# Feed-forward stream of a hybrid encoder layer: four inner tiles per PSUM sum, weights in 512-column units, a sixth of the low parts on GpSimd

## The chip, the cores and the metric

The kernel runs on one core of one Trainium2 chip. The metric is the device time of one execution in microseconds, and the time that is given is the median of several executions. The engines are TensorE (PE in the profile, with its weight loads as PEld), VectorE (DVE), ScalarE (ACT), GpSimd (POOL) and SyncE (SP), which issues the DMAs.

## What is computed

One layer: a feed-forward block, a mixing block with two kinds of attention side by side, a second feed-forward block, each between two RMS norms. All in float32.

```python
h = x + 0.5 * post1(SwiGLU_1(pre1(x)))
u = pre_mix(h)                      # multi-head latent attention and stick-breaking attention
h = h + post_mix(mix(u))            # 8 heads each, then one output projection
h = h + 0.5 * post2(SwiGLU_2(pre2(h)));  y = final(h)

def swiglu(x, w_gate, w_up, w_down):
    return (jax.nn.silu(x @ w_gate) * (x @ w_up)) @ w_down
```

D_MODEL is 1024, D_FF is 2816 (22 tiles of 128), and there are 1088 tokens: a prompt of 1024 and a sample of 64.

## The kernel before

The tokens are split into two groups: G1 with 576 tokens, moved through TensorE in two chunks of 288 columns, and G2 with 512 tokens in one chunk. Features lie on the partitions. Each float32 value is split into a high part that TensorE takes as it is (type float32r) and a low part, the rest; `mm3` (lines 159 to 162) computes one product as three matmuls, high by high, high by low and low by high. For weights the split is done on the chip: `weight` (lines 235 to 243) allocates a low and a high tile of 1024 columns, and for each half of 512 columns loads the raw values by DMA from SP's queue, casts them to the high part on ScalarE (line 121, `wh<-wr`) and subtracts on VectorE (line 122, `wl<-wr,wh`).

Two streams share TensorE. The feed-forward stream is `ffn` (lines 245 to 303), a generator that yields after each small step. The mixing stream is norms, projections, attention and the output projection. `weave` (lines 148 to 156) runs steps of the mixing stream and, in a ratio set stage by stage (`SHARE`, line 42), puts feed-forward steps between them. A planner then fixes the order of each engine's queue at build time by simulating the program with its own durations; each engine runs its queue in that order.

The order of work: the feed-forward block 1 of G1 alone; then mixing of G1 beside block 1 of G2; mixing of G2 beside block 2 of G1; then block 2 of G2 and the last norms. So `ffn` runs four times.

Inside `ffn` the 22 inner tiles are walked in parts of two. For an inner tile, the gate product (8 contraction tiles by 3 matmuls for each chunk) and the up product fill one PSUM bank each; ScalarE and VectorE form the silu (lines 289 to 293), and the result is split into `hh` and `hl`. The second product, `down`, runs one inner tile late, between the first and the second tile of the next part: it loads the two weight rows of the part, and for each of the 8 output tiles and each chunk sums the two inner tiles in a PSUM bank, six matmuls. The bank then goes into `y`: a copy on ScalarE in the first part (line 263), and an add on VectorE in the other ten parts (line 265, `y<-f,y`).

The feed-forward stream has four PSUM banks (`f`). Its SBUF ring is set in line 811: four raw tiles of 512 columns, four low and four high weight tiles of 1024 columns, three tiles each for `hh` and `hl`. The mixing stream has tiles of its own; its scores lie in one PSUM tile `s`, which is freed when the softmax or the scans of the stick-breaking weights (lines 520, 526 and 529, VectorE) have read it.

GpSimd does every second split of normalised inputs (line 122, `xl`, `ul`), some residual adds (line 234) and small memsets for the attention (lines 561, 562, 665, 711).

Of the kernel before, what the change touches and what calls it, by code (L numbers as in the profile page):

```python
# [7 lines left out]
F32 = mybir.dt.float32  # L8
# [7 lines left out]
P = 128  # L16
# [18 lines left out]
# token groups: (first token, tokens, chunk of the moving axis). The tokens lie as  # L35
# the first half of the prompt, the sample, the second half of the prompt.
# [4 lines left out]
# TensorE work of the feed-forward stream for one unit of the mixing stream's, part by part  # L41
# [8 lines left out]
class Layer:  # L50
    def __init__(self, tc, ctx, a):
# [33 lines left out]
        # keys and values: group 1 (prompt | new), group 2, cached  # L85
# [28 lines left out]
    # x = hi + lo exactly; without x, lo holds the value and is replaced in place  # L114
# [12 lines left out]
    # TensorE work is counted, for the interleaving of the two streams  # L127
# [15 lines left out]
    # a step without TensorE work in the first stream makes room for some of the second's  # L143
# [4 lines left out]
    # the steps of the first stream, with the second one's between them: self.share of its work each  # L148
# [15 lines left out]
    # a bank of the feed-forward stream  # L164
# [3 lines left out]
    # a bank of the mixing stream  # L168
# [10 lines left out]
    # sum of squares, tile by tile  # L179
# [9 lines left out]
    # 1 / sqrt(mean over all features + eps), on every partition, from the sums of squares  # L189
# [9 lines left out]
    # the same with the sums over the tiles left to TensorE (T at most 512)  # L199
# [10 lines left out]
    # tmp() gives [P, T] tiles  # L210
# [9 lines left out]
    # hi and lo of gain * src * r  # L220
# [7 lines left out]
    # y := res + gain * y * r, for one tile of features  # L228
# [15 lines left out]

    def ffn(self, pool, tmp, n, g, xhi, xlo, y, end=None, tail=None):
        nc, a = self.nc, self.a
        _, T, C = g
        wg, wu, wd = a[f"wg{n}"], a[f"wu{n}"], a[f"wd{n}"]
        pend = []
        order = [(dt, c0, C) for dt in range(KT) for c0 in range(0, T, C)]  # L250

        def down(part, first, order, beside=iter(())):
            ws = [self.weight(pool, wd[mi]) for mi, _, _ in part]
            for dt, c0, C in order:
                ps = self.bank_f()
                for i, ((wh, wl), (_, hh, hl)) in enumerate(zip(ws, part)):
                    self.mm3(ps[:, :C], wh[:, dt * P:dt * P + P], wl[:, dt * P:dt * P + P],
                             hh[:, c0:c0 + C], hl[:, c0:c0 + C], i == 0, i == len(part) - 1)
                yield True
                next(beside, None)  # L260
                yy = y[:, dt, c0:c0 + C]
                if first:
                    nc.scalar.copy(yy, ps[:, :C])
                else:
                    nc.vector.tensor_tensor(yy, ps[:, :C], yy, op=ALU.add)  # L265

        for m in range(0, FT, 2):
            part = []
            for mi in (m, m + 1):
                if mi > m and pend:  # L270
                    yield from down(pend.pop(0), m == 2, order)
                gh, gl = self.weight(pool, wg[mi])
                uh, ul = self.weight(pool, wu[mi])
                hh = pool.tile([P, T], F32R, name="hh")
                hl = pool.tile([P, T], F32R, name="hl")
                for c0 in range(0, T, C):
                    cs = slice(c0, c0 + C)
                    pg = self.bank_f()
                    for k in range(KT):
                        ks = slice(k * P, k * P + P)  # L280
                        self.mm3(pg[:, :C], gh[:, ks], gl[:, ks], xhi[:, k, cs], xlo[:, k, cs], k == 0, k == KT - 1)
                        yield True
                    pu = self.bank_f()
                    for k in range(KT):
                        ks = slice(k * P, k * P + P)
                        self.mm3(pu[:, :C], uh[:, ks], ul[:, ks], xhi[:, k, cs], xlo[:, k, cs], k == 0, k == KT - 1)
                        yield True
# [12 lines left out]
        if tail:  # L300
            order = [(dt, c0, tail) for c0 in range(0, T, tail) for dt in range(KT)]
        yield from down(pend.pop(0), False, order, end)
        self.run(end)

    # projections of the mixing block for the tokens of one group
    def project(self, gi, g, hi, lo, pool, ev, tmp):
# [14 lines left out]
        # query latent  # L321
# [13 lines left out]
        # rotary key: rows 64..95 the key, rows 96..127 its halves swapped  # L335
# [14 lines left out]
        # stick-breaking queries and keys, two heads per tile  # L350
# [16 lines left out]
        # latent attention: queries  # L367
        for m in range(2):
            # four heads: [query tile][head][128]
# [12 lines left out]
        # key/value latent  # L382
# [14 lines left out]
        # stick-breaking values, tokens on the partitions  # L397
# [17 lines left out]
        # latent attention: keys and values  # L415
# [3 lines left out]
    def cached(self, pool, ev, tmp):  # L419
        """keys and values of the cached latents"""  # L420
        nc, a = self.nc, self.a
        wh, wl = self.weight(pool, a["wukv"])
        cal = ev.tile([P, PAST], F32R, name="ll")
        cah = ev.tile([P, PAST], F32R, name="lh")
        ca = tmp()[:, :PAST]
        nc.sync.dma_start(ca, a["c_lat"])
        self.split(cah, cal, x=ca)
        yield from self.latent_kv(ev, tmp, wh, wl, cah, cal, PAST, PAST, 2)
# [25 lines left out]
    # ---- attention pieces  # L454
    def load_keys(self, pool, kind, h, parts):
        """hi and lo of the keys of one head on 128 rows."""
# [19 lines left out]
    def load_values(self, pool, pair, parts):  # L476
        """[128 keys, key tile, head, hi|lo, 64]"""
# [620 lines left out]
```

## Time and profile before

| what | value |
|---|---|
| median of three runs | 2368.2 us |
| the three runs | 2366.61, 2368.2 and 2371.72 us |
| span of the profiled execution | 2367.6 us |
| TensorE busy | 2283.5 us, 96% |
| VectorE busy | 1539.0 us, 65% |
| ScalarE busy | 1244.7 us, 53% |
| GpSimd busy | 93.6 us |
| mean granted TensorE clock | 0.993 of full speed |

The profiled execution has no time listed beside its span of 2367.6 us, from the first to the last instruction; the span lies inside the range of the three runs. The profile is one execution. Busy time of an engine is the union of its instructions; waits are idle time just before an instruction, put down to what released it last. A busy TensorE is not one at its peak, since matmuls overlap.

### The profile page before, as it was taken

To read this page: it belongs to the slowest core of one execution; us is meant where nothing else is said; L and a number is where in the kernel's file an instruction comes from. 1 tells how busy PE (TensorE), PEld (TensorE's weight loads), DVE (VectorE), ACT (ScalarE), POOL (GpSimd) and SP (SyncE) were. 2 spreads that over 40 slices of the span, in tenths; PEclk is the share of its full clock that TensorE was granted. 3 is DMA by queue.
4 is the path that set the end of the run, shared out by engine and by line. 5 is a ranking of instruction groups with operands and counts; after the bars stand their busy time and mean duration, and the time that the engine had idled before them with its cause. 6 is when DMAs were issued, how large, how long until landed. Compare 5 with 4: busy or idle time off the path is not lost.

```text
span 2367.6 us, 37687 instructions
## 1 busy us (share of the span) xinstructions
PE 2283.5 (96%) x13869; PEld 2033.4 (86%) x13869; DVE 1539.0 (65%) x2743; ACT 1244.7 (53%) x2459; POOL 93.6 (4%) x270
## 2 busy tenths in 40 slices
PE   8999999989999999999999999999999999999997
PEld 7999999879987777788778999998888888888885
DVE  5555555764277878855873488888878588555555
ACT  6543333453367777754542477777776455433333
POOL 1000000010000000000110000000000010000001
PEclk9999999999999999999999999999999999999998
DMA  6322222445453343343444632323221424333321
GB/s 210 97 95 90 81 80 90 148 144 168 161 150 113 110 129 100 95 151 111 151 142 160 188 96 79 99 72 99 72 86 62 144 81 139 128 98 98 98 90 36
DMA packets 186615, 268.81 MB, mean 114 GB/s; under 512 B 59216, under 2 KB 68048, under 8 KB 186400
## 3 DMA queue, kind: packets, MB, share of 16 engines
q1 hardware_dynamic: 186432, 266.41, 35.8%
q8 instruction: 110, 1.80, 0.3%
q14 instruction: 73, 0.60, 0.1%
HBM read 227.61 MB, written 40.88 MB: 113 GB/s over the span
## 4 chain that ended last, share of the span: by engine, by line
PE 69%; DVE 12%; ACT 9%; DMA 4%; issue 4%; SPq 1%; POOL 1%; DVEq 0%; ACTq 0%; POOLq 0%
PE f L133 46%; PE s L133 11%; PE v L133 6%; PE t L133 3%; PE t L137 2%; DVE a L526 2%; DVE a L529 1%; ACT wh L121 1%; DVE a L520 1%; ACT a L517 1%; DVE wl L122 1%; ACT a L518 1%; ACT a L519 1%; DVE y L265 1%; DVE e L224 1%
## 5 line engine op out<-in xcount | busy, mean ns | idle before, releaser
L133 PE MATMUL f<-xh,wh 128*128 128x288 f32 (+1 forms) x2112 | 695.3, 329 | 4.4 <-ACT xh L121 2.8
L133 PE MATMUL f<-xl,wh 128*128 128x288 f32 (+1 forms) x2112 | 694.3, 329 | 2.9 <-POOL xl L122 1.8
L133 PE MATMUL f<-xh,wl 128*128 128x288 f32 (+1 forms) x2112 | 692.8, 328 | 0.0
L121 ACT CAST wh<-wr 128x512 fp32r<-128x512 f32 x638 | 374.2, 617 | 524.9 <-PE f L133 376.5
L122 DVE TENSOR_TENSOR wl<-wr,wh 128x512 fp32r<-128x512 f32 x638 | 431.2, 698 | 233.0 <-ACT wh L121 208.7
L133 PEld LDWEIGHTS f<-xl,wh 128*128 128x128 f32 x2112 | 397.7, 188 | 33.7 <-POOL xl L122 3.4
L133 PEld LDWEIGHTS f<-xh,wh 128*128 128x128 f32 x2112 | 397.6, 188 | 33.3 <-ACT xh L121 3.3
L133 PEld LDWEIGHTS f<-xh,wl 128*128 128x128 f32 x2112 | 397.5, 188 | 28.1 <-issue 0.8
L133 PE MATMUL f<-hh,wh 128*128 128x288 f32 (+2 forms) x1072 | 350.7, 328 | 6.6 <-ACT hh L121 3.2
L133 PE MATMUL f<-hl,wh 128*128 128x288 f32 (+2 forms) x1072 | 350.7, 327 | 0.0
L133 PE MATMUL f<-hh,wl 128*128 128x288 f32 (+2 forms) x1072 | 349.9, 327 | 0.2 <-DVE wl L122 0.2
L265 DVE TENSOR_TENSOR y<-f,y 128x288 f32<-128x288 f32 (+2 forms) x488 | 247.9, 523 | 85.4 <-PE f L133 83.8
L133 PEld LDWEIGHTS f<-hh,wh 128*128 128x128 f32 x1072 | 201.7, 189 | 23.4 <-ACT hh L121 4.0
L133 PEld LDWEIGHTS f<-hh,wl 128*128 128x128 f32 x1072 | 202.1, 189 | 14.3 <-issue 1.0
L133 PEld LDWEIGHTS f<-hl,wh 128*128 128x128 f32 x1072 | 202.1, 189 | 13.8 <-issue 0.8
L293 DVE TENSOR_TENSOR act<-f,act 128x288 f32<-128x288 f32 (+1 forms) x132 | 70.0, 531 | 92.6 <-PE f L133 91.8
L564 DVE TENSOR_TENSOR pl<-t,ph 128x384 fp32r<-128x384 f32 (+1 forms) x160 | 101.2, 633 | 35.6 <-ACT ph L563 31.2
L563 ACT CAST ph<-t 128x384 fp32r<-128x384 f32 (+1 forms) x160 | 86.7, 542 | 57.2 <-PE t L137 54.7
L292 DVE TENSOR_TENSOR act<-f,act 128x288 f32<-128x288 f32 (+1 forms) x132 | 69.8, 529 | 66.5 <-ACT act L291 66.4
L137 PE MATMUL t<-c_ident,a 128*128 128x128 f32 x616 | 106.0, 277 | 2.7 <-ACT a L531 0.9
L133 PE MATMUL s<-kh,qh 128*128 128x256 f32 (+3 forms) x224 | 84.4, 378 | 24.0 <-DVE a L529 16.1
L121 ACT CAST hh<-act 128x288 fp32r<-128x288 f32 (+1 forms) x132 | 64.8, 491 | 66.0 <-DVE act L293 65.9
(312 smaller groups left out, 3464.7 us busy)
## 6 DMA issues: line engine op xcount, KB each, us to landing
wr<-in_wg SPq DMA_DIRECT2D x176, 256.0 KB, 2.9
wr<-in_wu SPq DMA_DIRECT2D x176, 256.0 KB, 3.0
wr<-in_wd SPq DMA_DIRECT2D x176, 256.0 KB, 3.2
wr<-in_win SPq DMA_DIRECT2D x44, 256.0 KB, 3.3
kl<-ks SPq DMA_DIRECT2D x64, 128.0 KB, 2.8
wr<-in_wout SPq DMA_DIRECT2D x32, 256.0 KB, 2.8
h<-y SPq DMA_DIRECT2D x16, 288.0 KB, 2.3
p<-in_xT SPq DMA_DIRECT2D x16, 256.0 KB, 3.4
```

Of the source, the lines that this page charges most:

```text
L121: nc.scalar.copy(hi, x)
L122: eng.tensor_tensor(lo, x, f(hi), op=ALU.subtract)
L133: self.nc.tensor.matmul(out, lhsT=lhsT, rhs=rhs, start=start, stop=stop)
L137: self.nc.tensor.transpose(out, x, ident)
L224: self.nc.vector.scalar_tensor_tensor(x, src(k), self.gain(name, k), r, op0=ALU.mult, op1=ALU.mult)
L265: nc.vector.tensor_tensor(yy, ps[:, :C], yy, op=ALU.add)
L292: nc.vector.tensor_tensor(s, pg[:, :C], s, op=ALU.mult)
L293: nc.vector.tensor_tensor(s, pu[:, :C], s, op=ALU.mult)
L517: nc.scalar.activation(av, z, AF.Abs)
L526: nc.vector.tensor_tensor_scan(a[:, j0:n - 1][:, ::-1], zz[:, ::-1], a[:, j0:n - 1][:, ::-1], BIG, op0=ALU.add, op1=ALU.subtract)
L563: nc.scalar.copy(ph[:, end:], tr[:, end:])
L564: nc.vector.tensor_tensor(pl[:, end:], tr[:, end:], f(ph[:, end:]), op=ALU.subtract)
```

## The change

`GROUP = 4`: the inner tiles are walked in parts of four (22 is five parts of four and one of two). A product of the second kind sums the four inner tiles of a part in one PSUM bank, with twelve matmuls, before the bank is added to `y`. It still runs between the first and the second tile of the next part, now half by half: four weight units of 512 columns for the output tiles 0 to 3, then four for 4 to 7. The last part has two inner tiles, as before, and is run by `down_last`.

Weights of the feed-forward stream are loaded by `unit`: one low tile, one high tile and one raw tile of 512 columns each. The ring has eight low and eight high tiles of 512 columns where it had four of 1024, and five tiles each for `hh` and `hl` where it had three.

The subtraction of a unit goes to GpSimd for the second half of the up weights of every odd inner tile (11 in a run of `ffn`) and for the fourth inner tile's unit in each half of `down` (10 in a run): 84 of 528 units over four runs. The mixing stream's weights keep `weight`.

`dynamic_dma_scratch_size=1024` is passed to the program's builder. Comments are taken out; line numbers below `GROUP` shift.

```diff
+GROUP = 4
+    def unit(self, pool, src, eng=None):
+        lo = pool.tile([P, 512], F32R, name="wl")
+        hi = pool.tile([P, 512], F32R, name="wh")
+        raw = pool.tile([P, 512], F32, name="wr")
+        self.nc.sync.dma_start(raw, src)
+        self.split(hi, lo, x=raw, eng=eng)
+        return hi, lo
...
-        def down(part, first, order, beside=iter(())):
-            ws = [self.weight(pool, wd[mi]) for mi, _, _ in part]
-            for dt, c0, C in order:
-                ps = self.bank_f()
-                for i, ((wh, wl), (_, hh, hl)) in enumerate(zip(ws, part)):
-                    self.mm3(ps[:, :C], wh[:, dt * P:dt * P + P], wl[:, dt * P:dt * P + P],
-                             hh[:, c0:c0 + C], hl[:, c0:c0 + C], i == 0, i == len(part) - 1)
-                yield True
-                next(beside, None)
-                yy = y[:, dt, c0:c0 + C]
-                if first:
-                    nc.scalar.copy(yy, ps[:, :C])
-                else:
-                    nc.vector.tensor_tensor(yy, ps[:, :C], yy, op=ALU.add)
+        def units(src, eng=None):
+            return [self.unit(pool, src[:, i:i + 512], e) for i, e in ((0, None), (512, eng))]
+
+        def product(part, ws, first, dt, c0, C):
+            ps = self.bank_f()
+            ks = slice(dt % H * P, dt % H * P + P)
+            for i, ((wh, wl), (_, hh, hl)) in enumerate(zip(ws, part)):
+                self.mm3(ps[:, :C], wh[:, ks], wl[:, ks], hh[:, c0:c0 + C], hl[:, c0:c0 + C],
+                         i == 0, i == len(part) - 1)
+            yield True
+            yy = y[:, dt, c0:c0 + C]
+            if first:
+                nc.scalar.copy(yy, ps[:, :C])
+            else:
+                nc.vector.tensor_tensor(yy, ps[:, :C], yy, op=ALU.add)
+
+        def down(part, first):
+            for half in range(2):
+                ws = [self.unit(pool, wd[mi][:, half * 512:half * 512 + 512], nc.gpsimd if i == 3 else None)
+                      for i, (mi, _, _) in enumerate(part)]
+                for dt in range(half * H, half * H + H):
+                    for c0 in range(0, T, C):
+                        yield from product(part, ws, first, dt, c0, C)
...
-        for m in range(0, FT, 2):
+        for m in range(0, FT, GROUP):
             part = []
-            for mi in (m, m + 1):
-                if mi > m and pend:
-                    yield from down(pend.pop(0), m == 2, order)
-                gh, gl = self.weight(pool, wg[mi])
-                uh, ul = self.weight(pool, wu[mi])
+            for mi in range(m, min(m + GROUP, FT)):
+                if mi == m + 1 and pend:
+                    yield from down(pend.pop(0), m == GROUP)
+                gw = units(wg[mi])
+                uw = units(wu[mi], nc.gpsimd if mi % 2 else None)
...
-    sizes = {"wr": 4, "wl": 4, "wh": 4, "hh": 3, "hl": 3}
+    sizes = {"wr": 4, "wl": 8, "wh": 8, "hh": GROUP + 1, "hl": GROUP + 1}
...
-    nc = bacc.Bacc("TRN2", target_bir_lowering=False, num_devices=1)
+    nc = bacc.Bacc("TRN2", target_bir_lowering=False, num_devices=1, dynamic_dma_scratch_size=1024)
```

## Rows read from the trace of the kernel before

**Rows 1.** The page's first part: busy time, share of the span, instructions.

```profile
PE 2283.5 (96%) x13869; PEld 2033.4 (86%) x13869; DVE 1539.0 (65%) x2743; ACT 1244.7 (53%) x2459; POOL 93.6 (4%) x270
```

**Rows 2.** Windows: from:to, length, busy us of each engine (instructions), PEclk, DMA, GB/s.

```profile
60.00:420.00 360.00, 360.00 (x2712) 359.46 (x2711) 191.60 (x378) 136.28 (x286) 5.28 (x4) 1.00 0.27 88
660.00:1020.00 360.00, 351.47 (x1807) 277.26 (x1805) 290.67 (x591) 262.09 (x597) 17.46 (x118) 1.00 0.39 115
1380.00:1860.00 480.00, 459.44 (x3261) 429.81 (x3260) 389.98 (x693) 340.53 (x607) 13.69 (x92) 1.00 0.28 87
2040.00:2280.00 240.00, 240.00 (x1061) 198.72 (x1060) 125.38 (x194) 81.12 (x144) 0.00 (x0) 1.00 0.30 96
```

**Rows 3.** Waits of TensorE in 660:1020 and 1380:1860: total us, times, longest.

```profile
PE s L133 <- DVE a L526: 6.5, 18, 0.6
...
PE s L133 <- DVE a L529: 15.8, 25, 2.0
PE f L133 <- DVE y L265: 0.4, 2, 0.3
```

**Rows 4.** Timeline of 1640:1655, VectorE and TensorE at one late scan: start, us, instruction.

```profile
1644.16 0.95 DVE L520 SCALAR_TENSOR_TENSOR a<-s,a 128x768 f32<-128x768 f32 x1
...
1645.37 0.75 DVE L606 SCALAR_TENSOR_TENSOR osq<-o,c_osg,osq 128x512 f32<-128x512 f32 x1
...
1647.22 1.01 DVE L529 TENSOR_TENSOR_SCAN a<-s,a 128x383 f32<-128x383 f32 x1
1648.14 1.16 DVE L265 TENSOR_TENSOR y<-f,y 128x288 f32<-128x288 f32 x3
...
1648.37 0.44 PE L133 MATMUL s<-kh,qh 128*128 128x448 f32 x1 [2.02 <-DVE a L529]
```

**Rows 5.** Groups by form: count, busy us, mean ns, idle before and its releaser.

```profile
L265 DVE TENSOR_TENSOR y<-f,y 128x288 f32<-128x288 f32 x320 | 139.1, 451 | 42.9 <-PE f L133 42.0
L265 DVE TENSOR_TENSOR y<-f,y 128x512 f32<-128x512 f32 x152 | 102.3, 684 | 38.6 <-PE f L133 38.0
L122 DVE TENSOR_TENSOR wl<-wr,wh 128x512 fp32r<-128x512 f32 x638 | 431.2, 698 | 233.0 <-ACT wh L121 208.7 <-DMA vs<-e 13.2 <-PE f L133 3.8
L133 PE MATMUL f<-hh,wh 128*128 128x288 f32 x704 | 209.4, 298 | 4.6 <-ACT hh L121 3.2 <-DVE y L265 0.9 <-DVE act L292 0.2
```

**Rows 6.** Windows of line 265 alone (VectorE busy us, instructions), the two attention stages.

```profile
660.00:1020.00 360.00, 37.72 (x56) 1.00 0.39 115
1380.00:1860.00 480.00, 51.62 (x122) 1.00 0.28 87
```

**Rows 7.** Windows of tile `wl` (PE, PEld, DVE busy us, instructions), the same stages.

```profile
660.00:1020.00 360.00, 129.21 (x326) 61.13 (x325) 54.41 (x81) 1.00 0.39 115
1380.00:1860.00 480.00, 210.56 (x710) 133.25 (x710) 61.29 (x92) 1.00 0.28 87
```

**Rows 8.** GpSimd's groups by form: two-input subtractions of 128x512.

```profile
L122 POOL TENSOR_TENSOR xl<-e,xh 128x512 fp32r<-128x512 f32 x4 | 6.2, 1554 | 17.1 <-ACT xh L121 17.1
L122 POOL TENSOR_TENSOR xl<-p,xh 128x512 fp32r<-128x512 f32 x4 | 5.3, 1320 | 88.0 <-ACT xh L121 88.0
```

**Rows 9.** Timeline of 1163:1168, GpSimd and VectorE.

```profile
1164.27 1.41 POOL L122 TENSOR_TENSOR xl<-tmp,xh 128x576 fp32r<-128x576 f32 x1 [3.01 <-ACT xh L121]
...
1163.79 0.68 DVE L265 TENSOR_TENSOR y<-f,y 128x512 f32<-128x512 f32 x1
1164.38 1.83 DVE L122 TENSOR_TENSOR wl<-wr,wh 128x512 fp32r<-128x512 f32 x1
...
1167.95 0.68 DVE L122 TENSOR_TENSOR wl<-wr,wh 128x512 fp32r<-128x512 f32 x1
```

**Rows 10.** Waits in GpSimd's queue in 660:1020, then the longest kind in 1380:1860.

```profile
POOL a L665 <- DVE a L520: 146.8, 28, 8.3
POOL ph L561 <- PE v L133: 37.5, 5, 14.4
...
POOL ph L561 <- PE v L133: 195.0, 24, 13.9
```

**Rows 11.** DMA issues: count, KB each, median us to landing.

```profile
wr<-in_wd SPq DMA_DIRECT2D x176, 256.0 KB, 3.2
```

More of the change, by code (lines that the diff above doesn't have):

```diff
@@ L248, in ffn @@
         wg, wu, wd = a[f"wg{n}"], a[f"wu{n}"], a[f"wd{n}"]
+        H = KT // 2
         pend = []
-        order = [(dt, c0, C) for dt in range(KT) for c0 in range(0, T, C)]
-        def down(part, first, order, beside=iter(())):
-            ws = [self.weight(pool, wd[mi]) for mi, _, _ in part]
-            for dt, c0, C in order:
-                ps = self.bank_f()
-                for i, ((wh, wl), (_, hh, hl)) in enumerate(zip(ws, part)):
-                    self.mm3(ps[:, :C], wh[:, dt * P:dt * P + P], wl[:, dt * P:dt * P + P],
-                             hh[:, c0:c0 + C], hl[:, c0:c0 + C], i == 0, i == len(part) - 1)
-                yield True
-                next(beside, None)
-                yy = y[:, dt, c0:c0 + C]
-                if first:
-                    nc.scalar.copy(yy, ps[:, :C])
-                else:
-                    nc.vector.tensor_tensor(yy, ps[:, :C], yy, op=ALU.add)
@@ new lines, in down, with down_last @@
+        def down(part, first):
[5 more added lines that the diff above has]
+                        yield from product(part, ws, first, dt, c0, C)
+        def down_last(part, step, beside):
+            ws = [[self.unit(pool, wd[mi][:, half * 512:half * 512 + 512]) for mi, _, _ in part] for half in range(2)]
+            if step:
+                order = [(dt, c0, step) for c0 in range(0, T, step) for dt in range(KT)]
+            else:
+                order = [(dt, c0, C) for dt in range(KT) for c0 in range(0, T, C)]
+            for dt, c0, n in order:
+                for _ in product(part, ws[dt // H], False, dt, c0, n):
+                    yield True
+                    next(beside, None)
@@ L278, in ffn @@
                     pg = self.bank_f()
[L279 to L282, printed above, removed]
                     pu = self.bank_f()
[L284 to L287, printed above, removed]
+                    for ps, ws in ((pg, gw), (pu, uw)):
+                        for k in range(KT):
+                            wh, wl = ws[k // H]
+                            ks = slice(k % H * P, k % H * P + P)
+                            self.mm3(ps[:, :C], wh[:, ks], wl[:, ks], xhi[:, k, cs], xlo[:, k, cs],
+                                     k == 0, k == KT - 1)
+                            yield True
                     s = tmp()[:, :C]
@@ L299, in ffn @@
         end = end() if end else iter(())
-        if tail:
-            order = [(dt, c0, tail) for c0 in range(0, T, tail) for dt in range(KT)]
-        yield from down(pend.pop(0), False, order, end)
+        yield from down_last(pend.pop(0), tail, end)
         self.run(end)
```

## The prediction

> **What bounds the kernel now.** I read the page's first part, then the windows by stage, then TensorE's waits in the stages where it is not full. The first says that TensorE is busy 96% of the span, 2283.5 of 2367.6 us, with VectorE at 65% [rows 1]. So all that any edit beside TensorE can give back is 84 us, unless the matmuls themselves become fewer, and they don't. The windows say where these 84 us lie: in the two stretches in which the feed-forward stream runs alone (60 to 420 and 2040 to 2280) TensorE is busy for every one of the 600 us [rows 2]. There nothing is to be had. In the attention stages it is busy 351.5 of 360 and 459.4 of 480 us, so 8.5 and 20.6 us are idle, 29.1 together [rows 2]; the remaining 55 us lie at the start, at the end and in the norms and projections between the stages.
>
> In the attention stages VectorE is the fullest engine after TensorE: 290.7 of 360 and 390.0 of 480 us, 81% in both [rows 2]. The waits name it: TensorE stood before the scores matmul, which needs the one tile `s`, until a scan of the stick-breaking weights had ended, for 6.5 and 15.8 us, 22.3 together [rows 3]. The timeline of one such wait shows how it arises. The scan of line 529 follows line 520, but VectorE does a headnorm multiplication of 0.75 us and other small work between them; the scan ends near 1648.2, three adds into `y` that had piled up follow at once, and TensorE has been standing for 2.02 us [rows 4]. VectorE's queue is late there, and TensorE pays, because its own order is fixed.
>
> **Part 1: half of the adds into y go.** Ten of eleven parts end in adds before, five of six after; the last part keeps its own. In two runs over G1, adds of 288 columns fall from 320 to 160; of G2's 152 adds of 512 columns, 80 go (block 1 has 80 and keeps 40, block 2 has 72 and keeps 32). That is 160 by 0.451 and 80 by 0.684 us, 72 and 55, together 127 us of VectorE's 1539 [rows 5]. The matmuls stay as many; only the place of start and stop moves. In the stretches without mixing this is hidden already: TensorE is full there, and the adds wait for TensorE, not it for them [rows 2, 5]. In the attention stages line 265 takes 37.7 and 51.6 us [rows 6], so 18.9 and 25.8 us go. A bank now lasts twelve matmuls instead of six before VectorE must empty it; TensorE's waits for that are only 0.4 us there [rows 3], so this is worth nothing by itself.
>
> **Part 2: 84 of 528 subtractions go to GpSimd.** VectorE loses 84 by 0.698, 59 us [rows 5]. GpSimd takes 1.32 to 1.55 us for the same shape [rows 8], so it gains 111 to 130 us on top of 93.6, which is little over a span of 2367. In the attention stages there are 81 and 92 such subtractions on VectorE [rows 7]; a sixth are 13 and 15, worth 9 and 10 us.
>
> Against this stands what the trace shows where both engines subtract at once. At 1164.27 GpSimd begins a subtraction of 1.41 us; the `wl` that VectorE begins at 1164.38 takes 1.83 us, where the same form alone takes 0.68 [rows 9]. The add into `y` just before it kept its 0.68 us. So a blocked piece costs VectorE up to 1.15 us more, against 0.7 saved. The bounds of a moved piece for VectorE are a gain of 0.70 (no meeting) and a loss of 0.45 (each one meets a `wl`). Units come in groups of four and are cast one behind the other, so meetings will be common; I take half, a gain of about 0.1 us a piece, and so nothing, and keep both ends for the range. The Trainium skill, in "SBUF — State Buffer", section "Who interferes with whom", gives this as a rule: a VectorE instruction with two SBUF inputs and a GpSimd instruction that reads SBUF exclude each other for the whole instruction. By that rule every such meeting would block, and those rows agree.
>
> GpSimd's queue is in order too, and behind its waits the moved piece would be late. It waits for the attention there, 5.2 us at a time on the commonest line (146.8 in 28), 14.4 at the longest [rows 10]. A group of four units of G2 lasts 48 matmuls at about 0.23 us, 11 us of TensorE's feed-forward work, and as that has some 70% of TensorE in this stage, an estimate from the timeline's pitch and the share of `f`, 16 us; a load (3.2 us [rows 11]), cast and subtraction take 5 of it. So 11 us are left, the usual wait fits, the longest misses by some 4 us. Cost 0 to 11 us (three misses); I take 0, since the usual wait is the nearest row. Queued behind a moved piece on GpSimd are the memsets for the attention; each may come up to 1.55 us later, and they run well before their readers.
>
> **Part 3: the rest.** Weights in units are the same bytes, loads, casts and subtractions; a unit's slots come free half a tile earlier, and nothing waits for it, so 0. SP's queue issues the same loads in the same number. Casts on ScalarE stay as many; copies of line 263 too. The first second product comes two inner tiles later: 0. A feed-forward step of twelve matmuls between mixing steps is coarser; its cost lies between a gain and a loss of about one step, 1.6 us, at each of the few stage changes, and I take 0. All instructions are planned anew, which shifts each queue a little: I give that 4 us either way, from the spread of 5.1 us that the three runs of one kernel have.
>
> **The sum.** In the attention stages VectorE's load falls by 18.9 + 9 and 25.8 + 10, less some 10 and 12 us for meetings (13 and 15 by about 0.8): to 273 of 360 and 366 of 480 us, 76% in both, from 81%. How waits shrink with that no row shows; between nothing (the waits come from chains that one engine runs in series) and all 22.3 us [rows 3]. As an estimate I take waits to go as load over idle share: 0.81/0.19 is 4.3, 0.76/0.24 is 3.2, a quarter less; without meetings (73%) a third. Of the 29.1 us idle [rows 2] this is 7 to 10, and I take 7. Start, end and stage changes: 0. The profiled span of 2367.6 lies 0.6 us under the median, so the forecast is 2368.2 - 7, 2361 us.
>
> What is late next is again the chain in VectorE's and ScalarE's queues behind one `s` tile: 520, 526 and 529 take some 3 us in series whatever else is queued [rows 4].
>
> **The rivals.**
>
> Nothing changes. TensorE is full where it was full, and the waits for the scans stay, since they come from scans that take longer than the planner believed, not from adds. For: in [rows 4] the adds stand behind the scan, not before it. Against: other pieces do stand between. Time 2368, give or take 4.
>
> A larger gain: the waits for the scans go altogether and the stage changes, which have VectorE chains too, shrink by some. 22.3 us less, 2346 us. For: both stages name VectorE almost alone [rows 3]. Against: the serial part of the chain stays.
>
> Slower: the meetings on the shared SBUF input. Place: the attention stages, 28 moved pieces, and the stage changes, where GpSimd has its large work. Price: if each blocked `wl` holds up the scan behind it for 1.15 us and TensorE waits for all of it, 32 us; less the 7 of the forecast, 25 us, 2393 us at the most; half of that is the likelier form, 2380. It decides when more than six of the 28 (7/1.15) hold up a scan on which TensorE waits. For: the stretch from 0.68 to 1.83 us is plain [rows 9]. Against: scans and adds read PSUM for one input, and the add beside GpSimd's work was not longer [rows 9], so only what stands directly behind a blocked piece suffers. It is the page's rule at its full price; by that rule alone, without the halved adds, the kernel would be slower.
>
> That the change does not do what it says: were the planner to bring GpSimd's pieces too late, TensorE would show waits for `wl` from GpSimd, up to 11 us; it is counted in the range.
>
> **How the numbers follow.** Forecast of a gain of 5 to 16 us: 0.42. Larger gain: 0.10. Nothing (within 0.2%, 4.7 us, which is about what a measurement can tell from no change here): 0.28. Slower: 0.20. So faster 0.52, same 0.28, slower 0.20. The likeliest case alone spans 2352 to 2363. The range for 8 in 10 leaves out most of the larger gain and the dear half of the slower case: 2349 to 2376.
>
> **What would show each step.** The group of line 265 with 248 instructions in all, and VectorE under 1400 us busy. GpSimd with 84 `wl` subtractions of 1.3 to 1.8 us, and single `wl` on VectorE of 1.2 to 1.9 us beside them. TensorE still full from 60 to 420. Its waits for lines 526 and 529 near 17 us instead of 22.3. I am wrong if VectorE's load in the attention stages falls as worked out and TensorE's idle time there does not; or if a wait of `f` for `wl` from GpSimd appears; or if the time moves in the stretches without mixing.

## The result, and the profile after

The changed kernel takes 2383.76 us (median of four runs, 2379.76 to 2386.27) where the kernel before takes 2368.24 (2366.61 to 2371.72): 15.5 us more, a ratio of 1.0058 with a 95% interval of 1.0044 to 1.0073. The profiled execution took 2381.92 us, with a span of 2380.1.

The first line of the page after, as in [rows 1]:

```profile
PE 2289.1 (96%) x13869; PEld 2036.3 (86%) x13869; DVE 1419.4 (60%) x2416; ACT 1267.6 (53%) x2462; POOL 206.7 (9%) x354
```

VectorE lost 119.6 us, and TensorE did not gain. For the same 13869 matmuls it is busy 5.6 us longer, and its idle time went from 84.1 to 91.0 us (span less busy time): 6.9 and 5.6 are the 12.5 us by which the two spans differ. What the 5.6 us are worth is taken up in the last section.

The windows after, columns as in [rows 2]:

```profile
60.00:420.00 360.00, 360.00 (x2714) 359.52 (x2713) 162.93 (x283) 143.12 (x291) 31.77 (x23) 1.00 0.28 88
660.00:1020.00 360.00, 349.98 (x1792) 273.81 (x1792) 267.03 (x541) 262.81 (x599) 34.57 (x131) 1.00 0.39 113
1380.00:1860.00 480.00, 458.76 (x3236) 427.14 (x3236) 361.83 (x611) 348.03 (x619) 30.24 (x105) 1.00 0.29 88
1860.00:2040.00 180.00, 168.06 (x910) 147.73 (x909) 119.78 (x187) 81.63 (x144) 23.23 (x15) 0.96 0.36 113
```

Where the feed-forward stream is alone, TensorE is still full. In the attention stages VectorE fell to 74 and 75%, and TensorE's idle time there rose, from 29.1 to 31.3 us. In the second stage change, from 1860 to 2040, TensorE is idle for 11.9 of 180 us, where the same window of before has 7.8; its granted clock there is 0.96 against 0.99, so more of that stretch stands at 1.2 GHz, the lower of its two levels. That window of before:

```profile
1860.00:2040.00 180.00, 172.18 (x919) 150.02 (x918) 126.30 (x203) 87.88 (x160) 12.65 (x8) 0.99 0.37 119
```

TensorE's longest waits after, over the whole span (total us, times, longest), then four of before:

```profile
PE s L136 <- DVE a L560: 15.4, 30, 1.1
...
PE s L136 <- DVE a L557: 6.3, 16, 0.7
PE f L136 <- DVE y L278: 6.2, 2, 5.9
PE s L136 <- DVE rx L190: 5.7, 1, 5.7
PE v L136 <- DVE tmp L190: 4.4, 2, 3.6
```

```profile
PE s L133 <- DVE a L529: 16.1, 26, 2.0
...
PE s L133 <- DVE a L526: 6.5, 18, 0.6
...
PE s L133 <- DVE rx L187: 2.2, 1, 2.2
PE v L133 <- DVE tmp L187: 2.2, 1, 2.2
```

The waits for the scans (lines 557 and 560 after, 526 and 529 before) are 21.7 us, and were 22.6; the 22.3 of [rows 3] leave out one wait of 0.3 us. What grew is single stalls at the stage changes: before a second-product matmul for an add into `y` (5.9 us), before the norm statistics `rx` (5.7) and `tmp` (3.6). The stall of 5.9 us in the timeline, VectorE first, then TensorE (start, us, instruction):

```profile
1933.55 0.46 DVE L278 TENSOR_TENSOR y<-f,y 128x288 f32<-128x288 f32 x1 [1.77 <-PE f L136]
1934.07 2.08 DVE L227 SCALAR_TENSOR_TENSOR e<-h,c_gains,rx 128x512 f32<-128x512 f32 x3
...
1939.19 3.08 DVE L227 SCALAR_TENSOR_TENSOR e<-h,c_gains,rx 128x512 f32<-128x512 f32 x3
...
1944.69 0.68 DVE L125 TENSOR_TENSOR xl<-e,xh 128x512 fp32r<-128x512 f32 x1
1945.30 1.54 DVE L278 TENSOR_TENSOR y<-f,y 128x288 f32<-128x288 f32 x4
...
1945.80 0.61 PE L136 MATMUL f<-hh,wh 128*128 128x288 f32 x1 [5.93 <-DVE y L278]
```

For eleven microseconds VectorE works through the scaling of the next norm (line 227 and its splits), which waits for GpSimd's splits in between. Four adds into `y` stand behind it in VectorE's queue, all four PSUM banks of the feed-forward stream are full, and TensorE stands.

### The profile page after: what moved, and what is told of

It reads as the page before. It is cut to its first block, busy times and chain, and to the rows that moved or that the text cites. A ratio compares the mean times of both kernels' runs of the same rounds, so it can differ in the third digit from the quotient of the medians.

```text
span 2380.1 us, 37747 instructions
## 1 busy us (share of the span) xinstructions
PE 2289.1 (96%) x13869; PEld 2036.3 (86%) x13869; DVE 1419.4 (60%) x2416; ACT 1267.6 (53%) x2462; POOL 206.7 (9%) x354
## 5 line engine op out<-in xcount | busy, mean ns | idle before, releaser
L124 ACT CAST wh<-wr 128x512 fp32r<-128x512 f32 x638 | 383.5, 618 | 507.1 <-PE f L136 343.3
L125 DVE TENSOR_TENSOR wl<-wr,wh 128x512 fp32r<-128x512 f32 x554 | 385.6, 709 | 242.9 <-ACT wh L124 206.2
L125 POOL TENSOR_TENSOR wl<-wr,wh 128x512 fp32r<-128x512 f32 x84 | 115.2, 1372 | 1136.0 <-ACT wh L124 1127.7
L136 PEld LDWEIGHTS f<-hl,wh 128*128 128x128 f32 x1072 | 202.4, 189 | 13.4 <-issue 0.5
L278 DVE TENSOR_TENSOR y<-f,y 128x288 f32<-128x288 f32 (+2 forms) x248 | 126.8, 519 | 109.1 <-PE f L136 108.5
L125 DVE TENSOR_TENSOR hl<-act,hh 128x288 fp32r<-128x288 f32 (+1 forms) x132 | 87.5, 663 | 43.0 <-ACT hh L124 42.5
```

What stands on the lines that cost most here:

```text
L124: nc.scalar.copy(hi, x)
L125: eng.tensor_tensor(lo, x, f(hi), op=ALU.subtract)
L136: self.nc.tensor.matmul(out, lhsT=lhsT, rhs=rhs, start=start, stop=stop)
```

## The experiments

Each run is beside runs of the kernel before on the same chip; "over before" is the difference of the two medians that were taken together. The kernel before had medians from 2367.3 to 2369.7 us on these occasions, so a difference between two runs of different occasions can shift by up to 2.4 us with the base that is used. e1 to e4 share one base, and so do e5 to e8, e9 and e10, e11 and e12, and e13 to e15.

| run | what it has | median, us | over before |
|---|---|---|---|
| the change | units, parts of four, GpSimd | 2383.8 | +15.5 |
| e2 | units, parts of two | 2379.0 | +11.6 |
| e1 | units, parts of four | 2370.0 | +2.7 |
| e3 | units, parts of two, GpSimd | 2392.0 | +24.6 |
| e4 | the change, other shares | 2384.9 | +17.6 |
| e5 | e1 and dummy subtractions on GpSimd | 2389.8 | +21.5 |
| e6 | e1 and memsets on GpSimd | 2377.0 | +8.7 |
| e7 | e1, GpSimd in the blocks alone | 2373.1 | +4.8 |
| e12 | e1, GpSimd beside mixing | 2383.4 | +13.7 |
| e8 | e2, adds first | 2371.8 | +3.5 |
| e9 | e1, adds first | 2371.1 | +3.8 |
| e10 | the change, adds first | 2376.3 | +9.0 |
| e11 | before, adds of 32 columns | 2378.2 | +8.5 |
| e13 | before, adds first | 2367.7 | -0.7 |
| e14 | e11, adds first | 2367.6 | -0.7 |
| e15 | e9, adds first at the residuals too | 2367.4 | -1.0 |

**The parts of the change.** Three runs take it apart: without GpSimd, with units alone, and with units and GpSimd but parts of two.

```diff
e1
-nc.gpsimd if i == 3 else None
-uw = units(wu[mi], nc.gpsimd if mi % 2 else None)
+None
+uw = units(wu[mi])
e2: e1 and
-GROUP = 4
+GROUP = 2
e3: the change and
-GROUP = 4
+GROUP = 2
-nc.gpsimd if i == 3 else None
+nc.gpsimd if i == 1 and half else None
```

> The changed kernel with its 84 subtractions back on VectorE; parts of four and units stay. Theory A (GpSimd's pieces hold up VectorE's two-input work in the serial chains at the stage changes; TensorE stands longer there and its clock falls to the lower level for some microseconds): 2366 to 2373 us, TensorE's stalls before rx and tmp at the stage changes (5.7 and 3.6 us in the changed kernel) back to about 2.3, granted clock at the lower level outside start and end for about 20 us instead of 24. Theory B (parts of four fall differently over the stage changes, so that adds into y queue behind the scaled chain and all four banks are full): still 2378 to 2386 us, with the 6 us stall before a second-product matmul near 1940 in place.

> Weights in units of 512 columns, but parts of two and nothing new on GpSimd. Theory A and B alike: within 0.2% of the kernel before, 2364 to 2373 us. If units themselves shift the plan so far that stalls move at the stage changes, it is off by more than 5 us, and neither theory is enough.

> Units, parts of two, and 84 subtractions on GpSimd (the up weights' second half of every odd inner tile, and the second inner tile's second half in the second product). Theory A: 2378 to 2386 us, as slow as the changed kernel. Theory B: 2364 to 2373 us, as the kernel before.

Without GpSimd: 2370.0 us, ratio 1.0011 (1.0001 to 1.0021). Units alone: 2379.0, ratio 1.0046 (1.0029 to 1.0063). Units and GpSimd with parts of two: 2392.0, ratio 1.0102 (1.0087 to 1.0117). So neither theory is enough. Units cost 11.6 us, parts of four on top of them give 8.9 back, and GpSimd costs 13.7 with parts of four (2383.8 against 2370.0) and 13.0 with parts of two. That these steps add up to about the 15.5 measured is no test, since each starts where the one before it ends; that GpSimd costs about as much with parts of two is one. Of Theory A's signs in e1, TensorE's wait before `tmp` is back at 2.1 us, but that before `rx` stays at 4.7 (2.2 before), and the granted clock from 1860 to 2040 at 0.96; so these two came in the main from something else than GpSimd's pieces.

Units alone were to change nothing. TensorE's wait in that run, and VectorE's queue ahead of it:

```profile
1929.94 0.46 DVE L278 TENSOR_TENSOR y<-f,y 128x288 f32<-128x288 f32 x1 [0.34 <-PE f L136]
...
1942.11 1.54 DVE L278 TENSOR_TENSOR y<-f,y 128x288 f32<-128x288 f32 x4
...
1942.62 0.61 PE L136 MATMUL f<-hh,wh 128*128 128x288 f32 x1 [9.53 <-DVE y L278]
```

It is the stall of the changed kernel, 9.5 us long. Eight adds stand behind the scaling here; in the kernel before, all but two of the sixteen are done when it begins. In the kernel before the same scaling meets another part of the feed-forward stream. The windows of the tiles `xh` (gate and up) and, of e2, `hh` (second product), from 1936 to 1942, columns as in [rows 2]; first before, then e2:

```profile
1936.00:1942.00 6.00, 6.00 (x32) 4.86 (x31) 2.99 (x3) 3.17 (x6) 3.15 (x3) 1.00 0.00 1
```

```profile
1936.00:1942.00 6.00, 0.00 (x0) 0.00 (x0) 0.00 (x0) 0.00 (x0) 0.53 0.00 0
```

Before, TensorE is full with gate and up products, whose banks last 24 matmuls each and need no add into `y`. In e2 it does nothing in these 6 us, and its granted clock is 0.53.

**Other shares.** The two shares of the attention stages were raised, to move the parts.

```diff
-SHARE = (0.1, 1.5, 0.1, 0.1, 1.2, 0.1)
+SHARE = (0.1, 1.6, 0.1, 0.1, 1.3, 0.1)
```

> The changed kernel with the shares of the feed-forward stream in the two attention stages at 1.6 and 1.3 instead of 1.5 and 1.2, so that parts of the feed-forward stream fall elsewhere over the stage changes. Theory A: 2378 to 2388 us, since the chains at the stage changes meet GpSimd's pieces anyway. Theory B: it moves by more than 5 us, to either side; the 6 us stall near 1940 is gone or is at another place.

2384.9 us, ratio 1.007 (1.0055 to 1.0085): the time did not move, and a stall of 5.2 us is there as before. TensorE's order did change, but only in the middle of the program; the part over the scaling stayed where it was. So the run speaks neither way.

**The adds first.** So the priority was changed instead: the feed-forward steps that are left are issued ahead of the scaling.

```diff
     def start2():
...
+        L.debt, L.pace = 96.0, 3.0
         yield from L.scaled(tmp, lambda k: h2[1][:, k], "pre2", rz[0], *x3)
+        L.pace = PACE
```

With units and parts of two (e8) TensorE's order stays as it is; VectorE takes eight adds into the scaled chain instead of behind it.

> Units with parts of two, and the feed-forward stream's remaining steps put ahead of the second norm's scaling (start2) in priority: on VectorE eight adds into y move from behind the scaled chain into it; TensorE's order stays. Theory B (units cost because a second product now lies over this chain and its four banks wait for the adds): the stall of 9.7 us is gone, and the time falls from 2379.0 to 2366 to 2371 us. Otherwise it stays at 2379.

2371.8 us, ratio 1.0012 (1.0002 to 1.0022): 7.2 us come back. VectorE in that run:

```profile
1937.62 0.69 DVE L125 TENSOR_TENSOR xl<-e,xh 128x512 fp32r<-128x512 f32 x1
1938.23 0.45 DVE L278 TENSOR_TENSOR y<-f,y 128x288 f32<-128x288 f32 x1
...
1939.92 1.17 DVE L278 TENSOR_TENSOR y<-f,y 128x288 f32<-128x288 f32 x3
...
1941.67 1.17 DVE L278 TENSOR_TENSOR y<-f,y 128x288 f32<-128x288 f32 x3
```

The adds are served in time, and no wait of `f` for `y` over 0.9 us is left in this stage change. 3.5 us of the units' cost stay unexplained.

The same line in three other kernels: parts of four without GpSimd (e9), the change (e10), and the kernel before as control (e13).

> Parts of four, units, nothing of the weights on GpSimd, and the feed-forward stream's remaining steps ahead of the second norm's scaling. If halving the adds is worth what the forecast said (7 us) once neither GpSimd nor the place of the second product costs anything: 2361 to 2365 us, faster than the kernel before by 0.1 to 0.3%, and 7 us under the units with parts of two in the same order (2371.8). If parts of four helped only because their banks fill more slowly under the scaled chain (9 us between 2379.0 and 2370.0), nothing is left of it: 2368 to 2372 us.

> The changed kernel with the feed-forward stream's remaining steps ahead of the second norm's scaling. The 6 us stall near 1940 goes: 2376 to 2380 us, and the distance to the same kernel without GpSimd's pieces stays 12 to 15 us if GpSimd's cost is spread over the other chains; if it sat in this one chain, both come out alike.

> The kernel before with the same priority for the remaining feed-forward steps ahead of the second norm's scaling. In it TensorE does gate and up products under that chain, so there is no stall of adds to take away. If the line helps only by that stall: 2364 to 2371 us, no change. If the line is a gain by itself: under 2362 us.

The control does not move: 2367.7, ratio 0.9998 (0.9989 to 1.0007). Parts of four come to 2371.1, ratio 1.0015 (1.0006 to 1.0024): no faster than e1, and where parts of two are with the same line. So the gain of 7 us does not come out. The time of e9 fits the second expectation, but not for the reason given there. TensorE's longest waits in this stage change of e1 show why:

```profile
1911.11 0.61 PE L136 MATMUL f<-hh,wh 128*128 128x288 f32 x1 [4.72 <-DVE y L278]
...
1939.96 0.58 PE L136 MATMUL f<-xh,wh 128*128 128x288 f32 x1 [2.90 <-DVE y L278]
```

In e1 the second product lies earlier than in e2 and in the change: most of it over the residual steps ahead of the norm, where TensorE waits for 4.7 us, and it ends 3 us after the scaling has begun. e9 has the same order of matmuls as e1. The new line takes its wait of 2.9 us away; the wait of 4.7 stays, and one of 4.2 for `hh` comes. So much of the 8.9 us that parts of four gave back is another place of the second product. A bank that lasts twice as long was compared only where that product lies over the scaling in both, with GpSimd's pieces: the stall is 9.5 us with parts of two (e3) and 5.9 with parts of four (the change). What halving the adds alone is worth in time stays open.

The change comes to 2376.3, ratio 1.0039 (1.0026 to 1.0053): 7.4 us less, and 5.2 over e9, not the 12 to 15 expected. From 1860 to 2040 TensorE is idle for 12.1 us in e9 and for 5.5 in e10, which keeps the change's order of matmuls and has none of e9's two long waits. So the 5.2 us understate GpSimd's pieces.

**GpSimd's share.** Dummy work on GpSimd, with all weights from VectorE: subtractions of the same operands that nobody reads (e5), or two memsets (e6).

```diff
-        self.split(hi, lo, x=raw, eng=eng)
+        self.split(hi, lo, x=raw)
+        if eng:
+            junk = pool.tile([P, 512], F32, name="junk")
+            eng.tensor_tensor(junk, raw, f(hi), op=ALU.subtract)
e6
+            eng.memset(junk, 0.0)
+            eng.memset(junk, 0.0)
```

> Parts of four, units, all subtractions back on VectorE, and GpSimd does 84 subtractions of the same operands into a spare tile that nobody reads. So GpSimd takes as long and reads as much as in the changed kernel, but no weight comes from it. Theory A (what costs is that VectorE's two-input instructions wait while GpSimd reads): 2380 to 2390 us, at least as slow as the changed kernel, since VectorE keeps its own 84 pieces too. Theory C (what costs is weights that come late from GpSimd's queue): 2367 to 2373 us, as the kernel with nothing on GpSimd (2370).

> As the dummy subtractions, but GpSimd writes two memsets of 512 columns each in their place and reads nothing. Theory A: 2367 to 2373 us, since nothing is read beside VectorE. If any work in GpSimd's queue costs (its own memsets for the attention come later, or the plan moves): 2376 us or more.

The dummy subtractions cost 19.8 us over e1 (2389.8, ratio 1.0085, 1.007 to 1.01), more than the real ones, though no weight waits for GpSimd. e5 has e1's order of matmuls, one for one, so neither late weights nor another order of TensorE is what costs there. VectorE's groups of e1, then of e5:

```profile
L125 DVE TENSOR_TENSOR wl<-wr,wh 128x512 fp32r<-128x512 f32 x638 | 437.1, 698 | 259.2 <-ACT wh L124 212.5 <-DMA vs<-e 21.2 <-PE f L136 15.1
L125 DVE TENSOR_TENSOR hl<-act,hh 128x288 fp32r<-128x288 f32 x88 | 40.9, 464 | 12.8 <-ACT hh L124 12.5
```

```profile
L125 DVE TENSOR_TENSOR wl<-wr,wh 128x512 fp32r<-128x512 f32 x638 | 473.6, 755 | 249.7 <-ACT wh L124 202.5 <-DMA vs<-e 21.2 <-PE f L136 15.5
L281 DVE TENSOR_TENSOR y<-f,y 128x288 f32<-128x288 f32 x160 | 70.9, 452 | 54.9 <-PE f L136 53.7
...
L125 DVE TENSOR_TENSOR hl<-act,hh 128x288 fp32r<-128x288 f32 x88 | 59.4, 675 | 12.5 <-ACT hh L124 12.3
```

The instructions with two SBUF inputs got longer, `wl` from 698 to 755 ns and `hl` from 464 to 675, while the add, which reads PSUM for one input, stayed at 452. VectorE is busy 1500.7 us in e5 and 1435.5 in e1: 65 us for 84 pieces, 0.78 us each. This is the rule of the Trainium skill weighed ahead ("SBUF — State Buffer", "Who interferes with whom"), and the rows agree with it.

The memsets are no even control. They depend on nothing, so the planner put them early: GpSimd is busy 43.7 of the first 60 us, and its busy time in the attention stages is that of e1. The first window of e1, then of e6:

```profile
0.00:60.00 60.00, 51.60 (x308) 46.19 (x309) 34.08 (x64) 36.40 (x80) 8.19 (x12) 0.94 0.64 207
```

```profile
0.00:60.00 60.00, 43.28 (x239) 37.66 (x240) 33.69 (x62) 35.20 (x77) 43.69 (x81) 0.91 0.61 196
```

TensorE loses 8.3 us there, which covers the 7 us by which e6 (2377.0, ratio 1.0034, 1.002 to 1.0048) is over e1. Its `wl` on VectorE takes 700 ns, as without them. Writes on GpSimd beside the attention were not tried.

Where the pieces cost: e7 has only those in the first and last block, which run mostly alone, e12 only those in the two blocks beside the mixing stream, 42 each.

```diff
+        gp = nc.gpsimd if (n == 1) == (T == 576) else None      # e7; e12 has != in place of ==
-nc.gpsimd if i == 3 else None
-uw = units(wu[mi], nc.gpsimd if mi % 2 else None)
+gp if i == 3 else None
+uw = units(wu[mi], gp if mi % 2 else None)
```

> The changed kernel with GpSimd's pieces only in the first and the last of the four feed-forward blocks, which run mostly without the mixing stream (42 of 84). Theory A with the cost in chains on which TensorE waits: 2368 to 2375 us, near the 2370 with none, because where the stream is alone VectorE has room. If each piece costs wherever it lies: about half of 13.7, 2377 us.

> The complement of GpSimd in the first and last block: the 42 pieces only in the two blocks that run beside the mixing stream. If the cost lies in chains on which TensorE waits: 2378 to 2384 us, nearly all of the 13.7 over the 2370 with none. If it were the same for every piece: 2377 us; if it were all in the blocks alone: 2370 us.

2373.1 (ratio 1.0017, 1.0007 to 1.0026) and 2383.4 us (1.0064, 1.0046 to 1.0082): 3.1 and 13.4 over e1, or 2.1 and 11.0 by the differences to before. So most of the cost comes with the pieces beside the mixing stream. The attention stages of e1, of e12 and of e5:

```profile
660.00:1020.00 360.00, 352.42 (x1817) 277.03 (x1817) 272.22 (x556) 262.99 (x599) 17.43 (x118) 1.00 0.39 114
1380.00:1860.00 480.00, 461.57 (x3266) 431.73 (x3265) 363.68 (x624) 347.01 (x616) 13.30 (x90) 1.00 0.29 89
```

```profile
660.00:1020.00 360.00, 349.02 (x1790) 273.05 (x1789) 266.69 (x540) 262.44 (x598) 34.73 (x131) 1.00 0.38 112
1380.00:1860.00 480.00, 458.98 (x3245) 427.65 (x3244) 362.31 (x613) 347.81 (x618) 30.68 (x107) 1.00 0.29 88
```

```profile
660.00:1020.00 360.00, 348.92 (x1787) 272.47 (x1786) 277.82 (x552) 262.42 (x598) 36.15 (x131) 1.00 0.39 112
1380.00:1860.00 480.00, 458.38 (x3256) 428.07 (x3255) 367.81 (x618) 344.04 (x611) 32.30 (x108) 1.00 0.27 83
```

TensorE is idle for 26.0 us there in e1 and for 32.0 in e12, though VectorE's load is slightly lower. e12's order of matmuls is not e1's, so a part of this may be the order's; but e5, which has e1's order, is idle for 32.7 us there with its dummies. Memsets for the attention that come late behind GpSimd's pieces, another rival, can be a small part only: VectorE waits for GpSimd for 1.1 us in these stages in e1 and 2.6 in e12, ScalarE in neither. From 1020 to 1380 TensorE is idle 2.8 us longer in e12, from 1860 to 2040 no longer (10.2 and 10.0 us). The other 4.3 us of the 13.3 by which the two spans differ are longer busy time of TensorE.

The pieces of the last block have a place of their own, one that e7 has too. In the changed kernel, GpSimd, then VectorE, then TensorE:

```profile
2004.44 1.75 POOL L125 TENSOR_TENSOR wl<-wr,wh 128x512 fp32r<-128x512 f32 x1 [4.37 <-ACT wh L124]
...
2003.68 0.75 DVE L190 TENSOR_TENSOR tmp<-tmp 128x576 f32<-128x576 f32 x1
...
2004.95 1.85 DVE L190 TENSOR_TENSOR tmp<-tmp 128x576 f32<-128x576 f32 x1
...
2012.39 0.85 PE L136 MATMUL v<-tmp,ones 128*128 128x288 f32 x1 [3.62 <-DVE tmp L190]
```

One step of the sum of squares on which TensorE waits takes 1.85 us instead of 0.75. The wait is 3.6 us here and in e7, and 2.2 in the kernel before and in e12.

**What VectorE's load is worth.** In the kernel before, each add into `y` was cut to 32 columns, alone (e11) and with the adds first (e14).

```diff
-                    nc.vector.tensor_tensor(yy, ps[:, :C], yy, op=ALU.add)
+                    nc.vector.tensor_tensor(yy[:, :32], ps[:, :32], yy[:, :32], op=ALU.add)
```

> The kernel before, with each add into y cut to its first 32 columns (the rest of the sum is left out), so that nearly all of the 248 us of VectorE in that line go, twice what the change takes out. If VectorE's load sets TensorE's waits, as the forecast had it: 2354 to 2360 us, waits for the two scans near 12 us instead of 22.6. If the waits come from the chain behind the one scores tile: 2364 to 2371 us, waits for the scans at 20 us or more.

> The kernel before with the adds into y cut to 32 columns (the rest of the sum is left out), and the remaining feed-forward steps ahead of the scaling. If the 9 us that the cut adds lost came from a second product lying over the scaled chain (a stall of 7.9 us): 2367 to 2371 us, and the load of VectorE is then worth nothing by itself. If VectorE's load were worth the forecast's 7 us or more: 2356 to 2362 us.

An add still takes 186 ns, so 161 us go rather than 248. Alone it is slower, 2378.2 us (ratio 1.0033, 1.0021 to 1.0045), with a stall for an add into `y` of 7.8 us under the scaled chain:

```profile
1935.77 0.61 PE L133 MATMUL f<-hh,wh 128*128 128x288 f32 x1 [7.77 <-DVE y L265]
```

With the adds first it is 2367.6 us (ratio 0.9995, 0.9983 to 1.0008), no faster than before as far as the interval tells; it leaves room for 4 us less, not for 7. TensorE's two waits for the scans and the attention stages of e14:

```profile
PE s L133 <- DVE a L529: 15.3, 28, 1.2
...
PE s L133 <- DVE a L526: 5.4, 15, 0.7
...
660.00:1020.00 360.00, 351.21 (x1814) 277.23 (x1813) 263.16 (x590) 258.28 (x597) 17.44 (x118) 1.00 0.39 115
1380.00:1860.00 480.00, 462.04 (x3240) 430.11 (x3239) 358.81 (x690) 344.51 (x607) 13.64 (x92) 1.00 0.29 88
```

VectorE is down to 73 and 75%, the waits for the scans are 20.7 us where they were 22.6, and TensorE is idle for 26.8 us in these stages where it was 29.1. Against these 2.3 us stand waits that the kernel before does not have, the longest of 4.3 us before `rx` and 3.7 for `wl`.

**The best version found.** e9 with the adds first also at the residual steps of the output projection, in both groups:

```diff
         self.rsqrt(bank, s1, T, D, s1)
+        self.debt += 90.0
         for k in range(KT):
```

> Parts of four, units, nothing of the weights on GpSimd, with the feed-forward stream's remaining steps ahead of the scaling and also of the residual steps of the output projection in both groups. If the two stalls of about 5 us that remain at the stage changes (before rx, and before a second product near 1908) come from adds and silu work that queue behind the residual chain: 2361 to 2366 us, under the kernel before. If the chains are then late themselves: 2368 to 2374 us.

2367.4 us, ratio 0.9996 (0.9987 to 1.0005): 3.7 us under e9, level with the kernel before and not under it. From 1860 to 2040 the longest wait for an add into `y` fell from 4.7 to 2.1 us and that for `hh` from 4.2 to 0.8. The wait before `rx` in the first stage change is still 4.9 us; what makes that chain late was not looked into. The time lies between the two expectations.

## Why the prediction was wrong

The forecast was 2361 us, a gain; the kernel is slower by 15.5, beyond the range. Step by step:

The count of the edits was right. Line 265 fell to 232 adds of full width and 16 of the tail; GpSimd does 84 subtractions of 1.37 us; and VectorE's load in the attention stages came to 74 and 75% where 76 was worked out. VectorE's own gain from the 84 pieces is 16 us (1435.5 in e1, 1419.4 in the change), 0.19 us a piece. Part 2 took a gain of about 0.1, but the sum then took off about 0.8 us a piece for meetings, which is a loss of 0.1; the two do not agree, and with half of the meetings throughout the loads come to 270 and 363 us. The measured 267.0 and 361.8 are nearer to that. VectorE under 1400 us was wrong by 19. No wait of `f` for `wl` from GpSimd appeared. But TensorE's idle time in the attention stages did not fall with VectorE's load, and that is the first sign of being wrong that the prediction named.

Three steps failed. Between the gain of 7 us and the loss of 15.5 lie 22.5 us: 9.7 are there without GpSimd (e1 is 2.7 over before), and 12.8 come with its pieces.

**The first step that failed is the sum's last: that TensorE's waits shrink with VectorE's load.** A quarter or a third less of 29.1 us was taken from a formula that no row bore out. e1 has just the load that was forecast, 272.2 and 363.7 us, and is idle for 26.0 us there: 3.1 less, not 7. In the change, with the load lower still, it is 31.3. The waits for the scans went from 22.6 to 21.7 us, and with two thirds of the adds' time gone (e14) to 20.7. So nearly all of them stay when 5 to 8% of VectorE is freed. That they come from the chain behind the single scores tile, as the first rival said, fits this and [rows 4], where the adds stand behind the scan; no run changed that chain.

**The second is "planned anew, 4 us either way".** The spread of runs of one kernel is no measure of what another plan costs. Units alone changed no work and cost 11.6 us; shorter adds in the kernel before, less work, cost 8.5. In both, a second product's adds came to stand behind the scaling of the next norm, a serial chain on VectorE, while its four banks filled. Taking those adds forward gives 7.2 and 10.6 us back, and does nothing to the kernel before, which has no such stall. So this term is worth some 10 us, and "start, end and stage changes: 0" was wrong with it. A bank that lasts twelve matmuls was priced at nothing beside the mixing stream; under this chain the stall is 5.9 us with it and 9.5 without (the change and e3). Why the adds came to stand there when the weights came in units was not settled. Earlier release of the slots is one guess; e2 also differs from the kernel before in that the bank of the up product is taken ahead of the gate product, and that the second product runs half by half.

**The third is GpSimd's pieces, taken at nothing.** The price of a meeting was right, but it was weighed in VectorE's busy time, where it nets to a small gain. It is paid in time that TensorE waits (idle for 81.2 us in e1 and 91.0 in the change): 13.7 us in the change, more than 5.2 once the adds go first, and 13.4 in e12 with the 42 pieces beside the mixing stream alone (12.8, and 11.0 in e12, by the differences to before). A part of each may be the other order of matmuls; that GpSimd's reads cost without one is shown by e5. The slower rival had this mechanism, and its likelier time, 2380 us, came near. That is luck in part: it priced waits for the scans, which did not grow (21.7 us in the change, 21.3 in e1), and had nothing for the stalls of the new plan. Its place was right in part: 5.3 us more idle time in the attention stages than in e1, some more in the stage changes. Which instruction's delay is paid for was not settled. `wl` on VectorE hardly lengthened on average (698 to 709 ns). `hl`, of 288 columns, went from 464 to 605 ns, but most of that lies between 60 and 420, where TensorE stays full, and in e12 it is 478. That weights come late from GpSimd's queue was rightly set at 0: the dummies, which deliver no weight, cost as much.

VectorE's and GpSimd's `wl` and VectorE's `hl` in the change; then the windows of the tile `hl` (TensorE, its weight loads, VectorE) of e1 and of the change:

```profile
L125 DVE TENSOR_TENSOR wl<-wr,wh 128x512 fp32r<-128x512 f32 x554 | 385.6, 709 | 242.9 <-ACT wh L124 206.2 <-DMA vs<-e 21.2 <-PE f L136 8.8
...
L125 POOL TENSOR_TENSOR wl<-wr,wh 128x512 fp32r<-128x512 f32 x84 | 115.2, 1372 | 1136.0 <-ACT wh L124 1127.7 <-ACT a L562 8.2
```

```profile
L125 DVE TENSOR_TENSOR hl<-act,hh 128x288 fp32r<-128x288 f32 x88 | 53.2, 605 | 28.6 <-ACT hh L124 28.5
```

```profile
60.00:420.00 360.00, 94.22 (x320) 60.02 (x320) 17.27 (x38) 1.00 0.28 88
```

```profile
60.00:420.00 360.00, 94.29 (x320) 60.07 (x320) 27.68 (x38) 1.00 0.28 88
```

## What to carry to other kernels

Work taken off a helper engine is worth only what the waits of the bounding engine lose, and that can be little: here 161 us less on VectorE took 2.3 us from TensorE's idle time in the attention stages and did not move the time measurably. Any edit to a kernel whose order is planned at build time moves the whole order; look at what lies over each serial chain before and after, and price that before the edit itself. Work for an engine whose reads hold up another is priced by what stands behind the blocked instruction, not by busy time.

## What was not expected of the hardware

Each of the 84 dummy subtractions of 1.51 us on GpSimd held VectorE up for 0.78 us on average, half of its length. And a stall costs more than its length: in e2 the granted clock had fallen to 0.53 in the 6 us in which TensorE stood, and in e11 the matmuls of 288 columns start every 0.13 us just before the stall of 7.8 us and every 0.24 us just after it (granted clock 0.59 from 1936 to 1940). The 5.6 us by which the changed kernel's TensorE was busy longer than the kernel before can't be put down to this: e13, which is as fast as the kernel before and has none of these stalls, was busy for 2287.9 us, 4.4 longer than it, at a mean granted clock of 0.988 against 0.993.
